# Step sizes and decays of a selective scan: their place in a two-layer diffusion block

## The chip, the core and the metric

The kernel runs on one core of a Trainium2 chip. The metric is the device time of one execution in microseconds (us), the median of several runs. Engines are named as in the profile: PE (TensorE's matmuls), PEld (its weight loads), DVE (VectorE), ACT (ScalarE), POOL (GpSimd), SP (the queue that issues most DMAs).

## What is computed

Two layers over 1024 latent tokens and 256 context tokens of width 1024. Each layer: modulated RMS norm, one input projection whose columns feed three head groups (latent attention, a bidirectional selective scan, windowed attention), one output projection, and a gated convolutional MLP. The part that matters here is the scan's:

```python
    xbc = jax.nn.silu(dwconv(xbc, conv_w, conv_b))
    xs, bm, cm = split_cols(xbc, (SSM_D_INNER, SSM_GROUPS * SSM_STATE, SSM_GROUPS * SSM_STATE))
    dt = jax.nn.softplus(dt_raw.astype(jnp.float32).reshape(b, l, 2, SSM_HEADS)
                         + dt_bias.astype(jnp.float32))
...
    xdt = (x.astype(f32) * dt[..., None]).reshape(b, nc, q, g, r, p)
    acs = jnp.cumsum((dt * a).reshape(b, nc, q, g, r), axis=2)
...
    a_last = acs[:, :, -1]
    states = jnp.einsum('bcqgn,bcqgr,bcqgrp->bcgrpn', bc, jnp.exp(a_last[:, :, None] - acs), xdt)

    def carry(hs, inp):
        st, al = inp
        return hs * jnp.exp(al)[..., None, None] + st, hs
...
    y_off = jnp.einsum('bcqgn,bcgrpn,bcqgr->bcqgrp', cc, h_start, jnp.exp(acs))
...
    y_diag = jnp.einsum('bcgqk,bcgrqk,bckgrp->bcqgrp', cb, decay, xdt)
```

Here `dt` are the step sizes, `acs` the decays summed within a chunk. There are 10 chunks of 128 tokens (2 of the context, 8 of the latent tokens), two directions and 6 heads: 12 step sizes per token. Everything runs in float32; matmuls of the projections are split into high and low halves, three products each.

## The kernel before

PE's instructions stand in the order in which the program text issues them. DVE, ACT, POOL and SP are ordered by the tile scheduler, which goes by a model of times. The text interleaves two streams: a *foreground* of projection products, and *background* generators. `bg(gen, delay)` queues a generator; each foreground product calls `tick()`, which resumes a generator when the modelled PE time has passed its due time; a `yield x` asks for x us of modelled PE time until the next resumption, with the numbers of the table `PACE` (one value for each layer). `drain()` runs what is left.

One layer's first half runs so in `body`:

- `w_in_ssd` (a generator) first makes the tile `krdt` (32 rows of a shared rotary key and 12 rows of raw step sizes, 1280 tokens wide) and the scan's gate `z`. Then it applies the rotary step in place to `krdt`: a shuffle L790 and a product L791 on DVE, a product L792 on POOL, the add L793 on DVE. It yields `krdt`.
- `next(w_in)` then makes the `xbc` columns: 7 groups of 128 channels, each a product over token chunks of 512, 512 and 256 (24 matmuls for each chunk, `p`), a convolution (DVE L508, ACT L512), transposes `ptr` and `px` and a spill to DRAM. In layer 0 the generator `early()` runs beside it: modulation vectors, long chains on DVE over tiles `wm` (L352, L354), transposes `pt` on PE, reductions L361. `drain()` ends this part, and the pool TD closes, whose place the scan's pool M takes.
- Then `side()` is queued as background: `ssd` (the scan), `scan_norm`, and `swa` (the windowed attention). The foreground goes on with `last_z` (the last columns of the gate), `w_in_att` (columns of the attentions), `mla_proj` (latent queries, keys, values) and `mla_att` (the heads of the latent attention).
- `drain()`, then `w_out` and the MLP.

`ssd` begins with the step sizes of all chunks: ten transposes `pdt` of `krdt`, the bias (L822), a softplus by a series on DVE (L828 to L839, with ACT's L825 and L826), a yield of 22, `dta` (L842), three matmuls `pacs` (the sums of the decays in both directions), copies L848 to L850, a yield, the transpose `pacT` and the DMA to `acsd` (L855), a few operations up to `wst` (L863), a yield, and then the scan: first the backward states (`xw` on POOL, L874, and the products `pst`), then for each chunk forward `pcb` and `py`. The results `dt`, `bias_`, `etot`, `wst` lie in a tile of pool M (tag "small"), the temporaries in a tile `sml2` of the pool U, which has 23 slots of 5 KB per partition.

Of the kernel before, what the change touches and what calls it, by code (L numbers as in the profile page):

```python
# [9 lines left out]
F32 = mybir.dt.float32  # L10
# [49 lines left out]
def _rope_tables():  # L60
# [21 lines left out]


PACE = {
    'dt': (22.0, 22.0),
    'back0': (4.0, 4.0),
    'back': (3.0, 3.0),
    'cb': (0.5, 0.5),
# [26 lines left out]
class Emit:  # L115
# [359 lines left out]

    def wk(self, w, M=128):
        return tuple([t[:, k, 0:M] for k in range(t.shape[1])] for t in w)

    def proj(self, w, x, chunks, M, put):

        ws = self.wk(w, M)
        for (s, e) in chunks:
            p = self.f("p")
            self.prod(ws, x, p[:M, 0:e - s], (s, e))
            put(p, s, e)

    def proj2(self, wps, x, chunks, need=None):

        for (s, e) in chunks:
            for ch in (CHUNKS[:1] if s == 0 else CHUNKS[1:]) if need else ():  # L490
                need(ch)
            ps = [self.f("p") for _ in wps]
            self.prods([self.wk(w, M) for w, M, _ in wps], x, [p[:M, 0:e - s] for p, (_, M, _) in zip(ps, wps)], (s, e))
            for p, (_, _, put) in zip(ps, wps):
# [65 lines left out]
    def up_names(self, l, u):  # L560
        return ("11", "12", "21", "22") if u < 2 else ("11", "12", "22", *(("21",) if l == 0 else ()), "S1", "S2", "S4", "S3")

    def up_weights(self, l):
# [10 lines left out]
        def make(u, name):  # L574
            def get():
# [8 lines left out]
                if name == "S1":  # L584
                    nc.vector.tensor_sub(a11, a11, a21)
                    nc.vector.tensor_add(a21, a21, a22)
                    raw = a21
                elif name == "S2":
                    nc.vector.tensor_sub(a22, a22, a11)
# [210 lines left out]
        return h, lo  # L800


    def ssd(self, l, krdt, out):
        nc, c = self.nc, l == 0
        sm = self.small[l]
        es = ExitStack()
        M = PoolTags(es.enter_context(self.tc.tile_pool(name=f"M{l}", bufs=1, reuse_waits="tile")),
                     {"small": 1, "fm": 2, "tm": 3, "ab": 4, "L": 3, "xw": 2, "cb": 2, "hf": 2, "hb": 2, "z": 2, "t": 1})
        S_ = M.tile([128, 4, 120], F32, tag="small", name=self.nm("sml"))
        dt, bias_, etot, wst = [S_[:, i, :] for i in range(4)]  # L810
        S2 = self.u(shape=[128, 10, 128], name="sml2")
        dta, tot, de, t1, av, t2 = [S2[:, i, 0:120] for i in range(6)]
        acs = de
        aexp, aT = S2[:, 6, 0:12], S2[0:120, 7, :]
        triF, triB = S2[:, 8, :], S2[:, 9, :]
        self.tri(triF, 0)
        self.tri(triB, 1)
        c3 = lambda ap: ap.rearrange("p (c j) -> p c j", j=12)
# [29 lines left out]
        nc.vector.tensor_copy(c3(acs)[:, :, 0:6], c3(p1[:, 0:120])[:, :, 0:6])  # L848
        nc.vector.tensor_copy(c3(acs)[:, :, 6:12], c3(p1[:, 120:240])[:, :, 6:12])
        nc.vector.tensor_copy(tot, p1[:, 240:360])  # L850
        yield 2.0
        p2 = self.b("pacT")
        self.tr(p2[:120, 0:128], acs)
        nc.vector.tensor_copy(aT, p2[:120, 0:128])
# [7 lines left out]
        nc.scalar.activation(etot, tot, AF.Exp)  # L862
        nc.vector.tensor_mul(wst, de, dt)  # L863

        yield 2.0

        def load_tm(k):
            t = M.tile([128, 5, 128], F32, tag="tm", name=self.nm("tm"))
# [3 lines left out]
        def weigh(tm, k, d):  # L872
            xw = M.tile([128, SH, SP], F32, tag="xw", name=self.nm("xw"))
            nc.gpsimd.tensor_tensor(out=xw, in0=tm[:, 0:3, :].rearrange("p i (h d) -> p (i h) d", d=SP),  # L874
                                    in1=c3(wst)[:, k, d * 6:d * 6 + 6].unsqueeze(2).to_broadcast([128, SH, SP]), op=ALU.mult)
            return xw
# [18 lines left out]
        xw = weigh(tms[0], order[0], 1)  # L895
        yield PACE['back0'][l]
        for i, k in enumerate(order):
            hn = M.tile([128, 384], F32, tag="hf", name=self.nm("hb"))
            tm, xk = tms.pop(0), xw
            if tms:  # L900
                xw = weigh(tms[0], order[i + 1], 1)
# [110 lines left out]
        hf = None  # L1012
# [5 lines left out]
        for i, k in enumerate(order):  # L1018
            hf = main(k, hf)
# [551 lines left out]
    def ffn(self, l, x, norm, feed, start=lambda: None, before_last=lambda: None):  # L1571
# [17 lines left out]
        def weight(u, name):  # L1589
            U_ = unit(u)  # L1590
            while name not in U_.w:
                U_.w[U_.names.pop(0)] = self.wnext(ahead=6)
            return U_.w[name]
# [24 lines left out]
        def step(u, s):  # L1618
# [22 lines left out]
            elif s == "6":  # L1641
                product(weight(u, "S2"), B["T2"], U_.X, False)
                put(U_, 0, 1, U_.X)
# [308 lines left out]
    def body(self):  # L1952
        tc, nc = self.tc, self.nc
        self.setup()
        self.C2 = PoolTags(self.ctx.enter_context(tc.tile_pool(name="c2", bufs=2)), {"r": 3, "vst": 1, "rr": 2, "edge": 2, "mx": 2, "mr": 2,
                             "sink": 1, "smx": 1, "smr": 1})
        self.W = PoolTags(self.ctx.enter_context(tc.tile_pool(name="W", bufs=2)), {"wst": 2, "whi": 3, "wlo": 3})
        self.U = PoolTags(self.ctx.enter_context(tc.tile_pool(name="U", bufs=2)), {"u": 23})
        self.PS = PoolTags(self.ctx.enter_context(tc.tile_pool(name="ps", bufs=2, space=PSUM)), {"f": 5, "b": 3})

        def xpool(l):
            es = ExitStack()
            p = es.enter_context(tc.tile_pool(name=f"X{l}", bufs=1, reuse_waits="tile"))
            self.X = PoolTags(p, {"x": 8, "ft": 1, "wm": 2, "pn": 1} if l == 0 else {"x": 9, "wm": 2})
            return es

        xs = xpool(0)
        self.wspec = self.layer_weights(0)
        x, h, need = self.start()
        for l in range(DEPTH):  # L1970
            c = l == 0
            chunks = CHUNKS if c else CHUNKS[:2]
            Y, hl, out = {}, {}, {}
            out["vst"] = self.C2.tile([128, NCH], F32, tag="vst", name=self.nm("vst"))
            self.zdone = False
            w_in = self.w_in_ssd(l, h, need)
            krdt = next(w_in)
            for f in range(KT):
                nc.sync.dma_start(out=self.spill[f], in_=x[f])
            xs.close()  # L1980
            with ExitStack() as es:
                self.TD = PoolTags(es.enter_context(tc.tile_pool(name=f"TD{l}", bufs=1, reuse_waits="tile")), {"t": 2, "tt": 2, "wm": 6})
                if c:
                    def early():
                        wt = lambda shape, name="wm": self.TD.tile(shape, F32, tag="wm", name=self.nm(name))
                        yield from self.mods_v(0, range(4, 12), wt, 3.0)
                        yield from self.load_params(1, wt)
                    self.bg(early())
                next(w_in)
                self.drain()  # L1990

            def side():
                self.scan = True
                yield from self.ssd(l, krdt, out)
                self.scan = False
                self.bg(self.scan_norm(l, Y, out["vst"]), PACE['sn0'][l])
                yield from self.swa(l, Y)
                while not self.ready:
                    yield 2.0
                for i in (6, 7):  # L2000
                    self.mix(l, Y, i, hl, i in (4, 1))

            self.ready, self.paced = False, True
            self.bg(side())
            next(w_in)()
            kva, qn = self.w_in_att(l, h)
            kbuf, qh, load, maxes = self.mla_loads(l)
            vt = self.mla_proj(l, kva, qn, kbuf, qh, load, maxes)

            def last():  # L2010
                self.ready = True
                for i in (3, 4, 5, 0, 1):
                    self.mix(l, Y, i, hl, i in (4, 1))

            finish = self.mla_att(l, vt, kbuf, qh, load, maxes, Y, last)
            self.drain()
            self.paced = False
            xs = xpool(l + 1)
            self.wspec = self.ffn_weights(l) + (self.layer_weights(l + 1) if l + 1 < DEPTH else [])
            x = []  # L2020
            norm = UpNorm(self, x, l, 1, chunks)
            self.w_out(l, Y, hl, finish, x, norm)
            x = []
            if l + 1 < DEPTH:
                tags = ["wm", "x"]

                def xw(shape):
                    tags.reverse()
                    return self.X.tile([128, NT] if tags[0] == "x" else [128, SEQ], F32, tag=tags[0], name=self.nm("wm"))[:, 0:SEQ].rearrange("p (k n) -> p k n", k=2)

                def xa(shape):
                    return self.X.tile(shape, F32, tag="wm", name=self.nm("wm"))

                def mods():
                    yield from self.mods_v(l + 1, range(12), xw, 4.6, xa, lambda n: 2 if n < 4 else 1)
                    self.gated = True

                self.gated = False
                nxt = Norm(self, x, l + 1, 0, CHUNKS, CHUNKS[:2])
                self.ffn(l, x, norm, nxt.feed, lambda: self.bg(mods(), 4.0), lambda: self.until(lambda: self.gated))  # L2040
                h, need = (nxt.hi, nxt.lo), nxt.need
            else:
                feed = self.final(x)
                self.ffn(l, x, norm, feed)
                self.drain()
        xs.close()
# [179 lines left out]
```

## Time and profile before

| | us |
|---|---|
| median of 3 runs | 3265.73 (3264.34 to 3267.45) |
| the profiled execution | 3266.09, of which the span is 3264.4 |
| PE busy | 3050.7 (93%) |
| DVE busy | 2132.6 (65%) |
| ACT busy | 1272.8 (39%) |
| POOL busy | 613.3 (19%) |

The profile is one execution. The span runs from the first to the last instruction; what is left of the execution's time, 1.7 us, lies around it. A share of the span is a mean over stages with different limits, so the rows below are read by stage. In rows of single instructions the bracket holds the idle time of that engine just ahead of the instruction, and what ended it. PEclk is the clock granted to TensorE, as a share of its full 2.4 GHz.

### The profile page before, as it was taken

What the parts mean: (1) busy time and instruction counts of PE and PEld (TensorE: products, weight loads), DVE (VectorE), ACT (ScalarE), POOL (GpSimd) and SP (SyncE); (2) the same over time, 40 slices, a digit from 0 to 9 for tenths busy, and PEclk for the clock granted to TensorE, in tenths of its full rate; (3) what the DMA queues carried; (4) which work ended last, traced back from release to release, by engine and by line L of the source; (5) the groups of instructions that cost most, each with busy time, mean ns of one, the idle gap of its engine ahead of it and who ended that gap; (6) DMA issues with size and microseconds to landing.
All of it is one profiled execution on the core that took longest, in us unless ns stands there. A gap on an engine that the chain in (4) does not pass through costs nothing.

```text
span 3264.4 us, 40114 instructions
## 1 busy us (share of the span) xinstructions
PE 3050.7 (93%) x15345; PEld 2402.0 (74%) x15345; DVE 2132.6 (65%) x3159; ACT 1272.8 (39%) x2204; POOL 613.3 (19%) x382
## 2 busy tenths in 40 slices
PE   6989978997999999997999999888999999999998
PEld 4878754554878888886888788655556778888887
DVE  4984887775285566668875734878653677677644
ACT  5433543443263343343111533553342444444212
POOL 2104633544100000000001303544453000000001
PEclk9989988998999999998999999988999999999999
DMA  8765666102202212227552445655113122225321
GB/s 269 221 188 156 211 216 173 39 15 95 96 30 73 79 58 71 78 67 285 176 166 78 130 115 164 215 173 149 42 42 97 62 78 78 90 84 180 130 74 62
DMA packets 349249, 392.42 MB, mean 120 GB/s; under 512 B 37203, under 2 KB 276452, under 8 KB 349057
## 3 DMA queue, kind: packets, MB, share of 16 engines
q1 hardware_dynamic: 348092, 389.62, 37.6%
q8 instruction: 121, 1.98, 0.3%
q0 software_dynamic: 704, 0.14, 0.1%
q14 instruction: 72, 0.58, 0.1%
q10 hardware_dynamic: 260, 0.10, 0.0%
HBM read 284.48 MB, written 104.01 MB: 119 GB/s over the span
## 4 chain that ended last, share of the span: by engine, by line
PE 77%; DVE 15%; DMA 3%; issue 2%; ACT 2%; POOL 1%; SPq 0%; DVEq 0%; ACTq 0%; POOLq 0%
PE p L143 34%; PE X L143 10%; PE Z L143 7%; PE s L143 6%; PE py L143 5%; PE pc L143 4%; PE V L143 3%; PE Y L143 3%; DVE wm L354 2%; DVE mx L1357 1%; PE pm L143 1%; PE pn L143 1%; PE pst L143 1%; DVE xbc L508 1%; DMA wm<-in_w_mod_dram 1%
## 5 line engine op out<-in xcount | busy, mean ns | idle before, releaser
L143 PE MATMUL p<-gh,wb 128*128 128x512 f32 (+1 forms) x1760 | 505.4, 371 | 0.0
L436 ACT CAST wb<-w 128x512 fp32r<-128x512 f32 (+1 forms) x412 | 251.5, 613 | 590.9 <-PE p L143 311.1
L437 DVE TENSOR_TENSOR wb<-w,wb 128x512 fp32r<-128x512 f32 (+1 forms) x412 | 279.4, 680 | 238.0 <-ACT wb L436 237.1
L143 PEld LDWEIGHTS p<-gh,wb 128*128 128x128 f32 x1760 | 321.1, 190 | 56.0 <-issue 0.2
L1567 DVE SCALAR_TENSOR_TENSOR x<-p,modT,x 128x512 f32<-128x512 f32 (+1 forms) x280 | 193.2, 695 | 243.8 <-PE p L143 243.5
L143 PE MATMUL X<-hb,wb 128*128 128x512 f32 x1440 | 340.4, 390 | 1.6 <-DVE cm L1605 1.6
L143 PE MATMUL p<-gl,wb 128*128 128x512 f32 (+1 forms) x880 | 325.7, 370 | 0.3 <-DVE gl L1746 0.3
L143 PEld LDWEIGHTS X<-hb,wb 128*128 128x128 f32 x1440 | 270.2, 188 | 58.3 <-DVE cm L1605 2.5
L143 PE MATMUL p<-hhi,wh 128*128 128x512 f32 (+1 forms) x792 | 290.9, 375 | 5.5 <-ACT z L643 3.3
L143 PE MATMUL p<-hlo,wh 128*128 128x512 f32 (+3 forms) x792 | 288.9, 366 | 2.6 <-POOL hlo L2128 1.8
L143 PE MATMUL p<-hhi,wl 128*128 128x512 f32 (+1 forms) x744 | 272.2, 366 | 2.5 <-DVE wl L424 2.3
L143 PE MATMUL Z<-hb,wb 128*128 128x512 f32 x960 | 233.0, 392 | 3.8 <-ACT cm L1607 3.8
L1441 ACT ACTIVATE P<-s 128x512 f32<-128x512 f32 x240 | 142.4, 597 | 239.5 <-PE s L143 236.1
L2074 POOL TENSOR_TENSOR acc<-acc,sq 128x512 f32<-128x512 f32 x24 | 32.8, 1371 | 1031.9 <-ACT sq L2073 1031.9
L143 PEld LDWEIGHTS Z<-hb,wb 128*128 128x128 f32 x960 | 180.1, 189 | 41.2 <-ACT cm L1607 4.7
L1448 POOL TENSOR_TENSOR acc<-acc,P 128x1024 f32<-128x1024 f32 x69 | 168.6, 2444 | 186.0 <-ACT P L1441 162.0
L143 PEld LDWEIGHTS p<-gl,wb 128*128 128x128 f32 x880 | 167.0, 190 | 28.1 <-DVE gl L1746 0.8
L354 DVE SCALAR_TENSOR_TENSOR wm<-wm,mstat,wm 128x512 f32<-128x512 f32 x224 | 161.6, 753 | 28.0 <-DMA wm<-in_w_mod_dram 27.5
L143 PEld LDWEIGHTS p<-hhi,wh 128*128 128x128 f32 x792 | 150.9, 191 | 31.2 <-ACT z L643 4.1
L143 PE MATMUL py<-P,vt 128*64 128x512 f32 (+3 forms) x744 | 173.4, 582 | 0.0
L143 PEld LDWEIGHTS p<-hlo,wh 128*128 128x128 f32 (+1 forms) x792 | 149.3, 188 | 26.0 <-POOL hlo L2128 2.7
L143 PEld LDWEIGHTS p<-hhi,wl 128*128 128x128 f32 x744 | 142.2, 191 | 26.5 <-DVE wl L424 3.2
(397 smaller groups left out, 5984.4 us busy)
## 6 DMA issues: line engine op xcount, KB each, us to landing
wm<-in_w_mod_dram SPq DMA_DIRECT2D x96, 512.0 KB
w<-in_ffn_w_up_dram SPq DMA_DIRECT2D x88, 512.0 KB
w<-in_ffn_w_down_dram SPq DMA_DIRECT2D x32, 512.0 KB
w<-in_w_in_dram SPq DMA_DIRECT2D x30, 512.0 KB
gd<-ft SPq DMA_DIRECT2D x22, 640.0 KB
gr<-gd SPq DMA_DIRECT2D x22, 640.0 KB
ab<-acsd SPq DMA_DIRECT2D x36, 384.0 KB
tm<-tmd SPq DMA_DIRECT2D x38, 320.0 KB
```

Of the source, the lines that this page charges most:

```text
L143: self.nc.tensor.matmul(out=out, lhsT=lhsT, rhs=rhs, start=start, stop=stop, **kw)
L354: nc.vector.scalar_tensor_tensor(out=acc[:, v, :], in0=w[:, i, :], scalar=c, in1=acc[:, v, :], op0=ALU.mult, op1=ALU.add)
L436: self.nc.scalar.copy(t[:, 0], raw)
L437: self.nc.vector.tensor_sub(t[:, 1], raw, t[:, 0])
L508: nc.vector.scalar_tensor_tensor(out=dst[:, d0:d1], in0=src, scalar=w, in1=dst[:, d0:d1], op0=ALU.mult, op1=ALU.add)
L1357: nc.vector.tensor_reduce(out=m[:, j, s:s + 1], in_=p, axis=AXX, op=ALU.max)
L1441: nc.scalar.activation(P[:, q * 512:(q + 1) * 512], s, AF.Exp, scale=sc)
L1448: (nc.vector if kt in ((2, 4, 6, 8) if self.scan else (4, 7)) else nc.gpsimd).tensor_add(acc, acc, P)
L1567: self.nc.vector.scalar_tensor_tensor(out=t[:, s:e], in0=p[:, 0:e - s], scalar=self.mcol(l, v, m)[:, o:o + 1], in1=t[:, s:e], op0=ALU.mult ...
L2074: (nc.gpsimd if self.n[ch] < 6 else nc.vector).tensor_add(acc, acc, sq[:, :n])
```

## The change

The part of `ssd` that makes step sizes and decays becomes a generator of its own, `ssd_dt`, and is queued as background ahead of the `xbc` columns of the same layer with a delay of 4. Its results go to a tile `sml` of pool U (instead of pool M), together with six of the former temporaries; two triangular masks and two small tiles stay in `sml2`, which is smaller. Two yields have new values (30 and 16 us for layers 0 and 1 in place of 22; 6 and 5 in place of 2), and the last yield of 2 is gone. `ssd` takes the results from `out["dt"]`.

```diff
 PACE = {
-    'dt': (22.0, 22.0),
+    'dt': (30.0, 16.0),
+    'dt2': (6.0, 5.0),
...
-    def ssd(self, l, krdt, out):
+    def ssd_dt(self, l, krdt, out):
+
         nc, c = self.nc, l == 0
         sm = self.small[l]
-        es = ExitStack()
-        M = PoolTags(es.enter_context(self.tc.tile_pool(name=f"M{l}", bufs=1, reuse_waits="tile")),
-                     {"small": 1, "fm": 2, "tm": 3, "ab": 4, "L": 3, "xw": 2, "cb": 2, "hf": 2, "hb": 2, "z": 2, "t": 1})
-        S_ = M.tile([128, 4, 120], F32, tag="small", name=self.nm("sml"))
-        dt, bias_, etot, wst = [S_[:, i, :] for i in range(4)]
-        S2 = self.u(shape=[128, 10, 128], name="sml2")
-        dta, tot, de, t1, av, t2 = [S2[:, i, 0:120] for i in range(6)]
+        S_ = self.u(shape=[128, 10, 128], name="sml")
+        dt, bias_, etot, wst, dta, tot, de, t1, av, t2 = [S_[:, i, 0:120] for i in range(10)]
+        out["dt"] = dt, bias_, etot, wst
+        S2 = self.u(shape=[128, 4, 128], name="sml2")
...
-        yield 2.0
+        yield PACE['dt2'][l]
...
         nc.vector.tensor_mul(wst, de, dt)
 
-        yield 2.0
+    def ssd(self, l, out):
+        nc, c = self.nc, l == 0
+        sm = self.small[l]
+        es = ExitStack()
+        M = PoolTags(es.enter_context(self.tc.tile_pool(name=f"M{l}", bufs=1, reuse_waits="tile")),
+                     {"fm": 2, "tm": 3, "ab": 4, "L": 3, "xw": 2, "cb": 2, "hf": 2, "hb": 2, "z": 2, "t": 1})
+        dt, bias_, etot, wst = out["dt"]
...
                     self.bg(early())
+                self.bg(self.ssd_dt(l, krdt, out), 4.0)
                 next(w_in)
                 self.drain()
 
             def side():
                 self.scan = True
-                yield from self.ssd(l, krdt, out)
+                yield from self.ssd(l, out)
```

Where the instructions stand. First PE in layer 0, where the first chunk of the `xbc` columns (`p_885`, 24 matmuls) ends; `krdt_461` is the tile of raw step sizes. Before:

```order
320 L143 MATMUL p_885<-hhi_581,wh_625 128x512
321 L143 MATMUL p_885<-hlo_582,wh_625 128x512
322 L143 MATMUL p_885<-hhi_581,wl_626 128x512
323 L143 MATMUL p_927<-hhi_396,wh_625 128x512
324 L143 MATMUL p_927<-hlo_397,wh_625 128x512
```

And in the changed kernel:

```order
320 L144 MATMUL p_885<-hhi_581,wh_625 128x512
321 L144 MATMUL p_885<-hlo_582,wh_625 128x512
322 L144 MATMUL p_885<-hhi_581,wl_626 128x512
323 L149 MATMUL pdt_927<-ident,krdt_461 128x44 x10
324 L144 MATMUL p_972<-hhi_396,wh_625 128x512
325 L144 MATMUL p_972<-hlo_397,wh_625 128x512
```

The ten transposes stood at row 839, behind the first matmuls of last_z; now they stand between the first two chunks of the columns. The matmuls `pacs` moved from row 951 to row 484, and `pacT` from 962 to 525.

Second, DVE at the same place. The row of `krdt_461<-krdt_461,sh_854` is the add that ends the rotary step. Before:

```order
101 L508 SCALAR_TENSOR_TENSOR xbc_877<-p_927,prm_172,xbc_877 128x511
102 L354 SCALAR_TENSOR_TENSOR wm_1040<-wm_1088,mstat,wm_1040 128x512 x2
103 L352 TENSOR_SCALAR wm_1200<-wm_1201,mstat 128x512 x2
104 L508 SCALAR_TENSOR_TENSOR xbc_877<-p_964,prm_172,xbc_877 128x255
105 L793 TENSOR_TENSOR krdt_461<-krdt_461,sh_854 32x1024
106 L508 SCALAR_TENSOR_TENSOR xbc_877<-p_927,prm_172,xbc_877 128x511
```

In the changed kernel, from the same place to the first operation on `pdt`:

```order
101 L355 SCALAR_TENSOR_TENSOR wm_1076<-wm_1127,mstat,wm_1076 128x512 x2
102 L353 TENSOR_SCALAR wm_1230<-wm_1231,mstat 128x512 x2
103 L794 TENSOR_TENSOR krdt_461<-krdt_461,sh_854 32x1024
104 L355 SCALAR_TENSOR_TENSOR wm_1076<-wm_1127,mstat,wm_1076 128x512 x2
105 L355 SCALAR_TENSOR_TENSOR wm_1230<-wm_1231,mstat,wm_1230 128x512 x2
106 L355 SCALAR_TENSOR_TENSOR wm_1076<-wm_1164,mstat,wm_1076 128x512
107 L800 TENSOR_TENSOR kpl_860<-krdt_461,kph_859 32x1280
108 L821 TENSOR_TENSOR sml_923<-pdt_927,sm_185 128x120
```

The two convolution operations at 101 and 104 moved behind the add; the chain of the step sizes begins at row 108 and ends with `dta` at row 199, with operations on `wm` between all of its steps.

Third, PE in layer 0 at the last forward chunk of the scan (its `pcb` is the third row of either listing). Before:

```order
1702 L143 MATMUL py_4040<-ab_3818,hb_3820 64x128 x2
1703 L143 MATMUL py_4040<-L_3879,tm_3812 64x128 x2
1704 L143 MATMUL pcb_4066<-fm_4017 128x128 x2
1705 L143 MATMUL pr_4090<-identr,mr_4006 1x128 x2
1706 L143 MATMUL s_4098<-qh_3343,kh_3339 128x512
```

In the changed kernel:

```order
1577 L144 MATMUL py_3718<-ab_3473,hb_3477 64x128 x2
1578 L144 MATMUL py_3718<-L_3529,tm_3469 64x128 x2
1579 L144 MATMUL pcb_3744<-fm_3690 128x128 x2
1580 L144 MATMUL pv_3762<-wh_3133,kvh_2317 128x384
1581 L144 MATMUL pv_3762<-wl_3134,kvh_2317 128x384
```

The last chunk stood directly ahead of the first scores of the latent attention (`s`); now products of `mla_proj` (`pv`, and `p` behind them) follow it.

## Rows read from the trace of the kernel before

**Rows 1.** Page, part 1 (busy us, share, instructions) and the chain of waits by engine.

```profile
PE 3050.7 (93%) x15345; PEld 2402.0 (74%) x15345; DVE 2132.6 (65%) x3159; ACT 1272.8 (39%) x2204; POOL 613.3 (19%) x382
...
PE 77%; DVE 15%; DMA 3%; issue 2%; ACT 2%; POOL 1%; SPq 0%; DVEq 0%; ACTq 0%; POOLq 0%
```

**Rows 2.** Busy time by stretch, layer 0's columns; the first line names the columns.

```profile
core 0: us, PE busy (x) PEld busy (x) DVE busy (x) ACT busy (x) POOL busy (x), PEclk, DMA share, GB/s
100.00:150.00 50.00, 49.15 (x268) 41.98 (x266) 50.00 (x81) 16.53 (x26) 6.41 (x3) 1.00 0.78 235
150.00:200.00 50.00, 49.58 (x279) 42.04 (x279) 50.00 (x91) 17.41 (x28) 0.00 (x0) 1.00 0.80 240
```

**Rows 3.** Tile `krdt` in layer 1: ns min/median/max, first and last start us.

```profile
L793 DVE TENSOR_TENSOR krdt<-krdt,sh x1: 1208/1208/1208, 1861.6 to 1861.6; 32x1024 f32<-32x1024 f32 x1
```

**Rows 4.** Single instructions, PE and DVE, layer 0: start, us, [idle before <-releaser].

```profile
103.01 0.39 PE L143 MATMUL p<-hhi,wl 128*128 128x512 f32 x1
103.24 0.39 PE L143 MATMUL p<-hhi,wh 128*128 128x512 f32 x1
...
118.36 1.20 DVE L793 TENSOR_TENSOR krdt<-krdt,sh 32x1024 f32<-32x1024 f32 x1
...
215.18 1.09 PE L148 MATMUL pt<-ident,wm 128*128 128x128 f32 x4 [6.64 <-DVE wm L354]
...
223.60 1.94 PE L148 MATMUL pt<-ident,wm 128*128 128x128 f32 x8 [6.48 <-DVE wm L354]
...
225.57 0.78 PE L143 MATMUL p<-hhi,wh 128*128 128x512 f32 x1
```

**Rows 5.** DVE groups by shape, 100 to 226 us: count, busy us, mean ns.

```profile
L354 DVE SCALAR_TENSOR_TENSOR wm<-wm,mstat,wm 128x512 f32<-128x512 f32 x101 | 71.6, 753 | 0.0
L508 DVE SCALAR_TENSOR_TENSOR xbc<-p,prm,xbc 128x511 f32<-128x511 f32 x28 | 20.4, 730 | 0.0
...
L361 DVE TENSOR_REDUCE modT<-pt 128x4 f32<-128x512 f32 x16 | 10.5, 672 | 0.8 <-PE pt L148 0.8
L508 DVE SCALAR_TENSOR_TENSOR xbc<-p,prm,xbc 128x255 f32<-128x255 f32 x14 | 6.5, 465 | 0.0
L352 DVE TENSOR_SCALAR wm<-wm,mstat 128x512 f32<-128x512 f32 x12 | 5.2, 467 | 0.0
```

**Rows 6.** Tile `sml`, 226 to 260 us; last, the POOL operation behind it.

```profile
L835 DVE TENSOR_TENSOR sml<-sml x9: 282/284/286, 232.6 to 237.2; 128x120 f32<-128x120 f32 x9
L836 DVE TENSOR_SCALAR sml<-sml x9: 222/223/224, 232.9 to 237.5; 128x120 f32<-128x120 f32 x9
...
L829 DVE RECIPROCAL sml<-sml x1: 890/890/890, 231.1 to 231.1; 128x120 f32<-128x120 f32 x1
...
258.54 2.60 POOL L874 TENSOR_TENSOR xw<-tm,sml 128x384 f32<-128x384 f32 x2 [37.36 <-DVE sml L863]
```

**Rows 7.** Busy time by stretch at the start of last_z.

```profile
225.00:231.00 6.00, 6.00 (x24) 4.67 (x23) 2.26 (x8) 2.12 (x4) 0.00 (x0) 0.50 0.91 311
231.00:240.00 9.00, 9.00 (x39) 7.39 (x38) 6.63 (x25) 1.65 (x2) 0.00 (x0) 0.96 0.02 6
```

**Rows 8.** Busy time by stretch: w_in_att, mla_proj, first heads, tail of layer 0.

```profile
261.00:350.00 89.00, 89.00 (x524) 76.40 (x523) 49.87 (x69) 35.83 (x79) 45.44 (x38) 0.96 0.58 165
370.00:450.00 80.00, 60.68 (x406) 50.36 (x404) 77.24 (x123) 43.55 (x115) 36.25 (x26) 0.91 0.79 249
450.00:490.00 40.00, 30.87 (x179) 21.41 (x179) 30.57 (x45) 16.73 (x32) 15.78 (x8) 0.83 0.55 169
490.00:510.00 20.00, 10.88 (x32) 5.61 (x33) 19.88 (x21) 6.13 (x9) 8.32 (x3) 0.57 0.75 256
740.00:765.00 25.00, 14.87 (x72) 8.33 (x70) 15.34 (x8) 11.49 (x17) 17.79 (x7) 0.80 0.00 1
```

**Rows 9.** Single PE instructions, tail of layer 0 and start of w_out.

```profile
760.90 1.12 PE L143 MATMUL pd<-acc,ones 128*64 128x512 f32 x2 [10.13 <-POOL acc L1178]
...
796.58 0.80 PE L143 MATMUL p<-mixh,wh 128*128 128x512 f32 x1 [6.42 <-ACT wh L423]
```

**Rows 10.** Layer 1: one PE instruction, then busy time by stretch (columns, scan).

```profile
1862.08 0.39 PE L143 MATMUL p<-hhi,wh 128*128 128x512 f32 x1
...
1900.00:1955.00 55.00, 55.00 (x289) 46.89 (x288) 20.13 (x35) 22.10 (x35) 0.00 (x0) 1.00 0.44 125
...
2050.00:2120.00 70.00, 57.81 (x363) 46.88 (x362) 57.23 (x85) 35.73 (x90) 38.59 (x26) 0.95 0.77 238
2120.00:2180.00 60.00, 51.38 (x304) 39.09 (x304) 48.30 (x87) 33.22 (x85) 24.75 (x16) 0.89 0.68 222
2180.00:2260.00 80.00, 67.92 (x286) 38.30 (x284) 62.40 (x76) 27.67 (x44) 35.87 (x15) 0.83 0.59 169
```

More of the change, by code (lines that the diff above doesn't have):

```diff
@@ L800, in split @@
         return h, lo
-    def ssd(self, l, krdt, out):
+    def ssd_dt(self, l, krdt, out):
         nc, c = self.nc, l == 0
         sm = self.small[l]
-        es = ExitStack()
-        M = PoolTags(es.enter_context(self.tc.tile_pool(name=f"M{l}", bufs=1, reuse_waits="tile")),
-                     {"small": 1, "fm": 2, "tm": 3, "ab": 4, "L": 3, "xw": 2, "cb": 2, "hf": 2, "hb": 2, "z": 2, "t": 1})
-        S_ = M.tile([128, 4, 120], F32, tag="small", name=self.nm("sml"))
-        dt, bias_, etot, wst = [S_[:, i, :] for i in range(4)]
-        S2 = self.u(shape=[128, 10, 128], name="sml2")
-        dta, tot, de, t1, av, t2 = [S2[:, i, 0:120] for i in range(6)]
+        S_ = self.u(shape=[128, 10, 128], name="sml")
+        dt, bias_, etot, wst, dta, tot, de, t1, av, t2 = [S_[:, i, 0:120] for i in range(10)]
+        out["dt"] = dt, bias_, etot, wst
+        S2 = self.u(shape=[128, 4, 128], name="sml2")
         acs = de
-        aexp, aT = S2[:, 6, 0:12], S2[0:120, 7, :]
-        triF, triB = S2[:, 8, :], S2[:, 9, :]
+        aexp, aT = S2[:, 0, 0:12], S2[0:120, 1, :]
+        triF, triB = S2[:, 2, :], S2[:, 3, :]
         self.tri(triF, 0)
@@ L863, in ssd @@
         nc.vector.tensor_mul(wst, de, dt)
-        yield 2.0
+    def ssd(self, l, out):
[5 more added lines that the diff above has]
+        dt, bias_, etot, wst = out["dt"]
+        c3 = lambda ap: ap.rearrange("p (c j) -> p c j", j=12)
         def load_tm(k):
```

## Prediction

> **What bounds the kernel now.** I read the engine shares first. TensorE (PE) is busy 93% of the span and the chain of waits is 77% PE [rows 1]: the kernel is one hand-written PE order, and a change is worth the PE idle time (and low granted clock) that it removes or makes. So I read PE's idle stretches and asked in each which engine ends the wait. Four places matter.
>
> First, the columns of layer 0's input projection. VectorE (DVE) is busy 50.00 us of every 50 there, with the modulation vectors of `early()`, while PE is dense at clock 1.00 [rows 2]. PE pays only at the end: two waits of 6.64 and 6.48 us, both ended by the last `wm` operations, and then a start of last_z at half clock [rows 4, 7]. Second, layer 0's scan beside mla_proj: 370 to 510 us, where DVE is nearly full and PE is idle for 37.6 of 140 us [rows 8]. Third, layer 0's tail, where PE waits 10.13 us for GpSimd's (POOL) accumulation and the clock is 0.80 [rows 8, 9]. Fourth, the same scan in layer 1: 2050 to 2260 us, with PE idle for 33 us at clocks of 0.95 to 0.83 [rows 10].
>
> **Where the step sizes go in layer 0: two new waits of PE.** PE runs its order strictly. In the trace four transposes wait 6.64 us with ready matmuls behind them, and nothing passes [rows 4]. The Trainium skill, page TensorE: Matmul & The Clock Gate, section The mechanism, says the same: matmuls start and end in program order. Were it otherwise the next two terms would be nearly nothing; the trace decides for the order.
>
> The ten transposes `pdt` stand right behind the first chunk of 24 matmuls. They read all 44 rows of `krdt`, and so they need the rotary step in place, whose last operation is the add L793 on DVE. PE begins the second chunk at 103.24 [rows 4]; the add starts at 118.36 and takes 1.20 [rows 4]. In the new DVE order two convolution operations ahead of it go behind it (0.73 + 0.47 us [rows 5]), because their matmuls now come later. So it ends at about 118.4, and PE waits 118.4 − 103.4 = 15 us. It could be 12 if the scheduler's order is kept more loosely, and no more than 16.
>
> Then DVE must run the chain of the step sizes among the modulation work. Between the add and `dta` the new order has 55 `wm` operations of 753 ns, 8 of 467, 8 + 4 convolution operations of 730 and 465, four reductions of 672 [rows 5], nine pairs of 284 + 222 and a reciprocal of 890 [rows 6], and some 6 us of others: 41.4 + 3.7 + 5.8 + 1.9 + 2.7 + 4.6 + 0.9 + 6 = 67 us. The durations of [rows 5] overlap by some 8% (they add up to about 136 us in a stretch of 126), so I take 62: `dta` ends at 118.4 + 62 = 180. PE gets to `pacs` after 153 matmuls, which last some 33 us at full clock, plus the transposes and a slow start: 118.6 + 1.3 + 33 + 3 = 156. It waits 24 us (15 if the durations are the short ones, 30 if they don't overlap).
>
> After a long wait the granted clock is 0.50 for about 6 us [rows 7], about 3 us of work each time, so 6 for two waits. On the other side the modulation work is done while PE waits: the last `wm` operation now stands ahead of the last two column groups, so the waits of 13.1 us at the end and the slow start there (3 us) go. Sum up to last_z: 15 + 24 + 6 − 13 − 3 = **+29 us** (+17 to +36). The ten transposes, three matmuls and one transpose only move.
>
> **What is queued behind.** Every column group waits with PE, and ScalarE's and DVE's convolutions after it. The scan's first state product needs `xw` from POOL, which needs the `tm` loads; these wait for the TD pool, which closes at the end of the columns. In the new order that product stands only some 5 us of matmuls behind last_z's start. I allow **+1.5 us** (0 to 3). POOL, which idled 37.36 us for the chain before [rows 6], is ready. The one DMA that moves, `acsd`, has no reader before the forward scan. The tile `sml` now holds one of 23 slots of the U pool through the scan; the rotation of w_in_att's tiles gets shorter by one. Nothing in the trace prices that; PE is dense there (89.00 of 89 us [rows 8]), so I take nothing, up to 5.
>
> **What is given back.** The scan no longer waits for its step sizes, so its chunks stand earlier against the foreground. Counting only projection matmuls from last_z on, at 0.227 us per 512 columns [rows 4], the first forward chunk stood at 58 us and now at 33, the last at 131 and now at 117. Each chunk now stands where the chunk three before it stood, and the last no longer sits at the very end of mla_proj with its partners bunched 6 and 4 us apart. In absolute time the scan starts as before (about 258); what is different is that some 28 us of w_in_att is still to be done then, which leaves DVE half free (49.87 of 89 us [rows 8]).
>
> *Layer 0, 370 to 510.* Idle 37.6 us; lost clock 0.09 × 60.7 + 0.17 × 30.9 + 0.43 × 10.9 = 15 us [rows 8]; together 53. Three chunks of ten leave it, at no gain for the rotations of the windowed attention at 490 to 510, which stay where they are. Somewhat under a third: **−16 us** (−4 to −26).
>
> *Layer 0's tail.* The windowed attention ends one head earlier, so that POOL's long sums stand further from the end. The wait of 10.13 and a little clock go: **−11 us** (0 to −14). What is late next is the 6.42 us wait for the weights of w_out [rows 9], which stays.
>
> *Layer 1.* No modulation work stands beside the columns: DVE is busy 20.13 of 55 us [rows 10]. The add of the rotary step starts at 1861.6 [rows 3], just as PE leaves its first chunk at about 1862 [rows 10]: a wait of 0.7 us, and up to 1 at `pacs`. There the shift is nearly free. 2050 to 2260 holds 33 us of idle and about 0.05 × 57.8 + 0.11 × 51.4 + 0.17 × 67.9 = 20 us of lost clock. A quarter of 53, less 1.5: **−12 us** (+2 to −22).
>
> **Sum:** +29 + 1.5 − 16 − 11 − 12 = −8.5 us against the profiled run's own 3266.09 (span 3264.4 and 1.7 around it; 0.4 above the median of 3265.73). That is 3257.
>
> **The rivals.** *Slower: the stalls of layer 0 are not won back.* Its place is PE's two waits behind DVE's modulation queue, its price the +29. It decides when the three later places together give back less than 30: if the chunks only trade with other DVE work, the mixer gives 5, the tail 8 and layer 1 5. That is 29 + 1.5 − 18 = +12.5, so 3279; with the longer second wait and w_in_att's tiles late, 3286. For it speaks that both waits are read from full DVE windows, while each gain is a share of a stretch with many waiters. *Faster by more:* the second wait is 15, the scan's stretches lose half of their loss in both layers: 20 + 1.5 − 26 − 12 − 22 = −38, so 3228. For it speaks that three of ten chunks go where DVE is half free. *No change:* the terms cancel to within 6.5 us, which is also about what a measurement tells from no change (0.2%); 3266. *It does not do what it says:* PE need not wait, because the new steps slip behind the modulation work; against it stands the written PE order, and it falls into the case before.
>
> **How the numbers follow.** Forecast 3257, with its neighbourhood from 3240 to 3259: 0.35. Slower: 0.28. Faster by more: 0.15. No change: 0.22. Faster 0.35 + 0.15 = 0.50, same 0.22, slower 0.28. The range holds the bounds with a tenth cut on either side: 3228 to 3286.
>
> **What would show it.** Right: in layer 0 PE waits about 15 us for `pdt`, ended by the add of `krdt`, and some 24 for `pacs`, ended by DVE; last_z starts near 254; no wait for `wm` at the end; less than 30 us of PE idle where the scan meets mla_proj; no 10 us wait for POOL in the tail; in layer 1 the two new waits are under 2 us. Wrong: the wait for `pacs` is under 10 or over 35 us, or the stretch beside mla_proj keeps its 38 us of idle, or the tail's wait comes back with another releaser.

## The result and the profile after

The changed kernel took 3311.34 us (median of 4 runs, 3310.12 to 3316.79) against 3265.52 for the kernel before: a ratio of 1.0138, 95% interval 1.012 to 1.0155. It is slower by 46 us, outside the range.

In the table, `last_z` and `w_out` stand for the first matmul of each, and the rotary step is the shuffle on `krdt`. All are start times in us of the two profiled executions.

| | before | after | later by |
|---|---|---|---|
| layer 0: last_z | 225.57 | 251.90 | 26.3 |
| layer 0: w_out | 796.6 | 839.1 | 42.5 |
| layer 1: rotary step of `krdt` | 1854.4 | 1895.6 | 41.2 |
| layer 1: w_out | 2470.6 | 2514.6 | 44.0 |
| end of the span | 3264.4 | 3308.9 | 44.5 |

So the loss is layer 0's, in two parts: 26.3 us up to last_z, where +29 was predicted, and 16 us from there to w_out, where −25.5 was predicted. Layer 1 loses 3 us in place of gaining 12.

The first part is as predicted, and answers [rows 4]. The page's engine line, PE's waits from 90 to 340 us (us in total, times, longest), and three stretches: one with the first wait in it, one with the second, and the 6.5 us behind the second:

```profile
PE 3054.6 (92%) x15345; PEld 2404.3 (73%) x15345; DVE 2126.1 (64%) x3156; ACT 1273.3 (38%) x2204; POOL 606.5 (18%) x385
```

```profile
PE pacs L144 <- DVE sml L856: 23.3, 1, 23.3
PE pdt L149 <- DVE krdt L794: 15.2, 1, 15.2
PE pst L144 <- POOL xw L880: 5.8, 1, 5.8
PE p L144 <- ACT z L644: 3.1, 1, 3.1
```

```profile
103.00:118.90 15.90, 0.69 (x4) 0.23 (x3) 15.90 (x21) 1.82 (x2) 5.34 (x3) 0.59 0.77 227
160.00:177.50 17.50, 0.03 (x1) 0.06 (x1) 16.12 (x36) 0.01 (x1) 0.00 (x0) 0.50 0.45 135
177.50:184.00 6.50, 6.50 (x27) 5.59 (x28) 6.17 (x14) 2.36 (x4) 0.00 (x0) 0.73 0.54 164
```

PE waits 15.2 us for the rotary add and 23.3 us for `dta` (L841, which ends at 177.3; the profile puts the wait down to L856, the next row of DVE), while DVE (the third busy column) is full or nearly so. Behind the second wait the granted clock is 0.73 for 6.5 us. The two waits for `wm` at the end are gone, and the first state product waits 5.8 us for its loads.

The second part is new. Whole stretch from last_z to w_out, before and then after (us, busy PE, PEld, DVE, ACT, POOL, PEclk, DMA share, GB/s):

```profile
225.50:796.60 571.10, 503.07 (x2744) 348.26 (x2742) 396.71 (x559) 247.89 (x486) 261.07 (x144) 0.93 0.43 130
```

```profile
251.90:839.10 587.20, 510.79 (x2726) 351.95 (x2725) 375.41 (x525) 240.33 (x478) 250.06 (x145) 0.92 0.42 128
```

The stretch is 16.1 us longer: 8.4 us more PE idle (76.4 in place of 68.0) and 7.7 more busy, for a little less work at a lower clock. DVE has 21 us less to do and still the gain didn't come. PE's waits from 456 to 516 us, where the scan ends beside mla_proj, say which one is new. Before:

```profile
PE pr L143 <- DVE sink L1059: 6.5, 1, 6.5
PE py L143 <- ACT z L998: 4.3, 1, 4.3
PE pm L143 <- DVE mx L1357: 1.7, 1, 1.7
```

After:

```profile
PE pm L144 <- DVE ql L1217: 11.3, 1, 11.3
PE pr L144 <- DVE mr L1369: 5.9, 1, 5.9
PE py L144 <- ACT z L1004: 4.0, 1, 4.0
PE pm L144 <- DVE vt L1295: 2.4, 1, 2.4
```

`ql` is the low half of a latent query, an operation of mla_proj. DVE's instructions ahead of it (start, us, [idle before <-releaser]), then PE's and ACT's at the same time:

```profile
491.03 0.69 DVE L1363 TENSOR_REDUCE mx<-pm 128x1 f32<-128x512 f32 x1 [0.51 <-PE pm L144]
494.72 0.01 DVE L791 LOAD_MASK_SELECT sh<-swr  x1 [3.00 <-DMA swr<-swd]
494.74 1.29 DVE L791 STREAM_SHUFFLE sh<-swr 128x1024 f32<-128x1024 f32 x1
496.06 1.23 DVE L792 TENSOR_TENSOR sh<-sh,sin 128x1024 f32<-128x1024 f32 x1
499.52 1.23 DVE L794 TENSOR_TENSOR swr<-swr,sh 128x1024 f32<-128x1024 f32 x1 [2.23 <-POOL swr L793]
502.07 1.49 DVE L1056 TENSOR_TENSOR swl<-swr,swh 128x1280 fp32r<-128x1280 f32 x1 [1.32 <-ACT swh L1055]
503.49 0.02 DVE L791 LOAD_MASK_SELECT sh<-swr  x1
503.49 1.28 DVE L791 STREAM_SHUFFLE sh<-swr 128x1024 f32<-128x1024 f32 x1
504.66 0.67 DVE L1217 TENSOR_TENSOR ql<-p,qh 64x512 fp32r<-64x512 f32 x1
```

```profile
493.82 0.28 PE L144 MATMUL p<-qn,wl 128*64 128x256 f32 x1
505.39 0.80 PE L144 MATMUL pm<-kh,qh 96*128 96x512 f32 x1 [11.29 <-DVE ql L1217]
```

```profile
500.78 1.26 ACT L1055 CAST swh<-swr 128x1280 fp32r<-128x1280 f32 x1 [8.75 <-DVE swr L794]
501.94 1.32 ACT L1216 CAST qh<-p 64x512 fp32r<-64x512 f32 x3
```

PE made the products for `ql` at about 493. DVE is idle for 6.5 us between 491 and 505, some 4 of them while PE waits, but `ql` stands in its queue behind a rotation of the windowed attention (the rotary step of a tile `swr` of its queries or keys), which waits in turn for a load, for POOL and for ACT. The same rotation holds ACT up: `qh`, the high half that `ql` reads, is cast only at 501.94, behind the cast of the rotated tile (`swh`), for which ACT was idle for 8.75 us. So `ql` stood behind the rotation in two queues, and PE waits for all of it. The loads (DMA share 0.84 from 483 to 506) come late too. Before the change the rotations began behind the last `ql`.

### The profile page after: what moved, and what is told of

Same layout as the page of the kernel before. It is cut to its first block, busy times and chain, and to the rows that moved or that the text cites. A ratio compares the mean times of both kernels' runs of the same rounds, so it can differ in the third digit from the quotient of the medians.

```text
span 3308.9 us, 40119 instructions
## 1 busy us (share of the span) xinstructions
PE 3054.6 (92%) x15345; PEld 2404.3 (73%) x15345; DVE 2126.1 (64%) x3156; ACT 1273.3 (38%) x2204; POOL 606.5 (18%) x385
## 4 chain that ended last, share of the span: by engine, by line
PE 77%; DVE 13%; DMA 4%; issue 3%; ACT 2%; POOL 1%; SPq 0%; DVEq 0%; POOLq 0%; ACTq 0%
PE p L144 34%; PE X L144 10%; PE Z L144 7%; PE s L144 5%; PE py L144 5%; PE pc L144 4%; PE V L144 3%; PE Y L144 3%; DVE wm L355 1%; DVE mx L1363 1%; PE pm L144 1%; PE pn L144 1%; DVE acc L1398 1%; DMA xr<-in_x_dram 1%; PE pst L144 1%
```

## The experiments

The theories were these. **A**: the loss is PE's two waits in layer 0's columns; the earlier scan costs (A1) or is neutral (A2). **B**: the slot of pool U that `sml` holds has a price. **C**, formed after the first eight runs (the expectation of `hold` had named the rotations under A1): the earlier scan pulls the rotations ahead of mla_proj's last operations on DVE. Times are medians; a ratio is to the kernel before on the same chip, with its 95% interval.

### Which layer

`l1only`: layer 0 makes the chain at the start of the scan again, with the old yields; `l0only`: layer 1 does.

```diff
...
-                self.bg(self.ssd_dt(l, krdt, out), 4.0)
+                if l == 1:
+                    self.bg(self.ssd_dt(l, krdt, out), (4.0, 4.0)[l])
...
+                if l == 0:
+                    yield from self.ssd_dt(l, krdt, out)
+                    yield 2.0
                 yield from self.ssd(l, out)
```

> Layer 0 makes its step sizes at the start of the scan again, with the old yields; layer 1 keeps them early; the tile sml is in pool U in both layers. Theory A (the loss is PE's two waits in layer 0's columns, and the earlier scan gives nothing back): layer 1's part alone is worth about +3 us, so 3265 to 3272. Theory B (the slot of pool U that sml holds slows the scan and the rotations of both layers): layer 0 keeps some 10 to 15 us of its loss too, so 3275 to 3285. My prediction's layer 1 term (-12) would give 3254.

> Layer 0 early as in the change, layer 1 at the start of the scan with the old yields; sml in pool U in both. Theory A: all but about 3 us of the loss stays, 3305 to 3310. Theory B: 3308 to 3315, since the slot is held in layer 1 as well. If layer 1's early chain itself loses, 3300.

`l1only`: 3277.37 us, 1.0034 (1.0023 to 1.0045). `l0only`: 3310.80, 1.0134 (1.0118 to 1.0149). Layer 0 holds nearly the whole loss. But 11 us stay without it, 8 of them in layer 0 up to w_out (804.7 against 796.6), where only the place of `sml` differs: more than A allows, and a first sign for B.

### The two waits

`late0`: layer 0's chain stands later within the columns.

```diff
-    'dt': (30.0, 16.0),
+    'dt': (70.0, 16.0),
...
-                self.bg(self.ssd_dt(l, krdt, out), 4.0)
+                self.bg(self.ssd_dt(l, krdt, out), (24.0, 4.0)[l])
```

> The change with layer 0's chain later within the columns: delay 24 in place of 4, first yield 70 in place of 30, so that PE meets pdt 20 us and pacs 54 us of projection matmuls later; layer 1 and the early scan as in the change. Theory A: both waits (15.2 and 23.3 us) go; VectorE's total work then ends the columns, about 10 us later than before the change; last_z starts near 236 in place of 251.9, and the time is 3292 to 3298. If the two waits were only a symptom, 3308 to 3313.

3291.23 us, 1.0080 (1.0057 to 1.0104). PE's waits from 90 to 250 us:

```profile
PE pacs L144 <- DVE sml L856: 11.8, 1, 11.8
PE pst L144 <- POOL xw L880: 5.9, 1, 5.9
PE pt L149 <- DVE wm L355: 4.5, 2, 3.1
```

The wait for `pdt` is gone; that for `pacs`, expected to go too, is halved. last_z starts at 232.5, 19.4 us earlier than in the change, and the time falls by 20.1 (19 by the ratios, whose interval here is 8 us to either side): what the columns lose arrives at the end about one for one. Of the 7 us that stay against 225.57, 3 are waits (11.8 for `pacs` and 4.5 for `wm`, where 13.1 stood before). 25 us of the loss stay, 18 of them behind last_z.

### The slot of pool U

`uslot`: the kernel before, with the tile in U instead of M. `copym`: the change, with a copy into M at the start of the scan. `late0copym`: `late0` with the same copy.

```diff
...
+        S_ = M.tile([128, 4, 120], F32, tag="small", name=self.nm("sml"))
+        nc.vector.tensor_copy(S_, out["sml"][:, 0:4, 0:120])
+        dt, bias_, etot, wst = [S_[:, i, :] for i in range(4)]
```

> The kernel before with one change: the tile of step sizes and decays lies in pool U (as in the change) and not in pool M; both layers make it at the start of the scan, with the old yields. PE's order is that of before, row for row. Theory B (the slot of U has a price of its own): by layer 0 of the run with only layer 1 early (8.1 us longer up to w_out than before) and layer 1 of the run with only layer 0 early (2.3 longer), 3274 to 3278. If the slot is free and those differences came from elsewhere: 3264 to 3268.

> The change, but at the start of the scan the four results are copied (one VectorE operation of 128 x 480) into a tile of pool M, and the slot of U is free from then on. Theory B: the slot's 8 + 2 us come back, 3299 to 3304. Theory A alone (waits and shift): 3309 to 3313, the copy's half microsecond at worst.

> As the run with layer 0's chain later in the columns (no waits of PE for pdt and pacs), with the copy into pool M as well. Theories A and B together: 3291 less the slot's 10, 3279 to 3284; what is then left over before (13 to 18 us) is 7 us of VectorE's longer queue in layer 0's columns and the price of the earlier scan. Theory A alone: 3289 to 3293. If the earlier scan were the gain that I predicted, the three together would come to 3250.

`uslot`: 3271.99 us, 1.0017 (1.0008 to 1.0026). `copym`: 3305.08, 1.0128 (1.0112 to 1.0143). `late0copym`: 3286.43, 1.0062 (1.0048 to 1.0076). By the ratios the slot costs 6, 3 and 6 us, less than the 10 that B expected. Only `uslot` against before is clear of its interval. In its profiled execution the loss lies in layer 0 (581.1 us from last_z to w_out against 571.0 before), while layer 1 is 4 us shorter. PE's order is that of before, but not all else is: the first cast of `qn` on ACT starts at 372.2 us in place of 365.7. What comes late for want of the slot was not followed further.

### The place of the scan

`hold`: the change with a yield of 26 ahead of the scan. `late0h13` and `late0h22`: `late0copym` with yields of 13 and 22 there. `l1m`: layer 0 as before, layer 1 early with the copy; `l1mhold`: the same with the scan of layer 1 held by 26.

```diff
+                yield (26.0, 26.0)[l]
                 yield from self.ssd(l, out)
```

> The change with a yield of 26 us of modelled PE time ahead of the scan in both layers, so that the scan's chunks stand against the foreground about where they stood before the change (first forward chunk 69 us of projection matmuls ahead of the first scores in layer 0, 72 before); the step sizes stay early. Theory A1 (the earlier scan pushes the rotations of the windowed attention into mla_proj and loses there): the two waits' +26 us stay and the rest goes, 3288 to 3296. Theory A2 (the earlier scan is neutral): 3305 to 3315. Theory B (slot of pool U): 3305 to 3312, since the slot is held even longer.

> The same base, with the scan held by 13 us of modelled PE time in both layers: half of the shift is undone, the last forward chunk stands 4 us of projection matmuls ahead of the first scores in layer 0 (14 in the change, 0 before). Theory A1 (the price grows with the shift, about 8 us in layer 0 and 3 to 5 in layer 1 for the half): 3277 to 3282. If the place of the scan is not what costs: 3284 to 3289.

> The same base with the scan held by 22 us: its forward chunks stand in layer 0 exactly where they stood before the change (72.4 us of projection matmuls ahead of the first scores down to 0). Theory A1: what is left is the 8 us by which last_z starts later, 3270 to 3277. If the place of the scan is not what costs: 3284 to 3289. The run that held the scan by 26 us, 3 us later than before, lost more in layer 0 than the shift did, which speaks for the second.

> Layer 0 exactly as before, layer 1 as in the change (early chain, early scan) but with the copy into pool M. Against the run that also held layer 1's scan (3265.8) it prices the earlier scan in layer 1 alone. My prediction: -12, 3254. Theory C: +3 to +6, 3268 to 3272. Neutral: 3264 to 3267.

> Layer 0 exactly as before; layer 1 with the early chain, the copy into pool M, and the scan held back by 26 us of modelled PE time, so that its chunks stand against the foreground where they stood before. What is left of the change is that ten microseconds of VectorE's chain and its two waits move from w_in_att into the columns of layer 1. Layer 1 was 6.4 us shorter than before in the run that held the scan. If that is the worth of the move, 3257 to 3261, faster than before; if it was chance of alignment, 3264 to 3268.

| | us | ratio (95%) |
|---|---|---|
| `hold` | 3301.85 | 1.0105 (1.0088 to 1.0122) |
| `late0copym`, no hold | 3286.43 | 1.0062 (1.0048 to 1.0076) |
| `late0h13` | 3271.01 | 1.0012 (1.0003 to 1.0022) |
| `late0h22` | 3282.94 | 1.0043 (1.0029 to 1.0057) |
| `l1m` | 3268.69 | 1.0006 (0.9996 to 1.0015) |
| `l1mhold` | 3265.80 | 1.0002 (0.9993 to 1.0011) |

In layer 1 the early chain is worth nothing, with its scan early or held. In layer 0 the place of the scan matters, by 15 us for a hold of 13, but not in one direction: A1's price growing with the shift falls, and A2 with it. `late0h22` is not settled: two of its ten executions, the profiled one among them, took 3268 to 3269 us, the others 3280 to 3286. I have no trace of the longer kind. `hold` fell into none of its three ranges and is no clean return either: its scan stood 3 us of matmuls later than before, its last `pcb` waited 9.8 us for a load, and it lost more behind last_z than the change (593.1 us to w_out against 587.2). In it the rotations begin at 518 us, well behind the last `ql` at 467, and PE waits 15.6 us in total for a result of the windowed attention (`smr`): a windowed attention that comes too late has a price too.

### The rotations

`late0sw`: `late0copym` with one line ahead of the windowed attention, which leaves the scan early. `aftsw`: the change itself with that line. `befsw`: the kernel before with it.

```diff
+                yield 26.0
                 yield from self.swa(l, Y)
```

> The run with the later chain and the copy, with a yield of 26 us of modelled PE time ahead of the windowed attention in both layers: the scan keeps its early place, the three rotations of the windowed attention go back behind mla_proj. Theory C (the early scan costs because the rotations' VectorE operations, waiting for swr loads and POOL, stand ahead of mla_proj's ql in VectorE's queue: 16.5 us of PE's waits for ql in that run): the waits for ql fall under 4 us, and the time to 3272 to 3281. If the rotations only pass the wait on to the heads (sink and mr, 13 us before the change), 3282 to 3290.

> The change itself with one line more: a yield of 26 us of modelled PE time ahead of the windowed attention in both layers. Chain, scan and the tile in pool U stay as in the change, and so do the waits of PE for pdt and pacs. Theory C (what was lost behind last_z is the rotations ahead of mla_proj's ql in VectorE's queue): about the 24.5 us that the same line gave on the base without the waits, 3285 to 3292; the waits for ql (11.3 + 3.1 us in layer 0) fall under 7. If the line only worked together with the later chain or the copy: 3300 to 3312.

> The kernel before with the same line ahead of the windowed attention, and nothing else. If the line were a gain of its own, whatever the step sizes do: 3240 to 3260. Theory C says that before the change the rotations stand behind mla_proj anyway, so that the line only delays the windowed attention into the end of the layer: 3266 to 3290.

`late0sw`: 3261.86 us, 0.9986 (0.9975 to 0.9996), 24.6 less than its base (25 by the ratios); C expected less of a gain, and a wait for `ql` under 4 us, where 6.5 stay. `aftsw`: 3286.81, 1.0073 (1.0058 to 1.0088), 24.5 less than the change (21 by the ratios). `befsw`: 3276.05, 1.0035 (1.0022 to 1.0047), 12.5 more than before. The line gains on two bases and loses where the rotations already stood behind mla_proj, so it is no gain of its own. It moves the whole windowed attention, not the rotations alone, and it does so in both layers. PE's waits in `aftsw` from 251 to 830 us:

```profile
PE pr L144 <- DVE mr L1369: 11.6, 5, 6.2
PE pd L144 <- POOL acc L1184: 10.4, 2, 10.1
PE p L144 <- ACT wh L424: 6.7, 1, 6.7
PE pst L144 <- POOL xw L880: 5.7, 1, 5.7
PE p L144 <- DVE ql L1217: 4.3, 1, 4.3
```

The change has a second, shorter wait for `ql` beside the one of 11.3 us:

```profile
PE p L144 <- DVE ql L1217: 3.1, 1, 3.1
```

So the waits for `ql` fall from 14.4 to 4.3 us. The wait of 10.1 us in the tail of [rows 9] is back. That the two gains are so near to each other is in part chance: in the profiled executions layer 0's stretch from last_z to w_out gets 13.3 us shorter in `aftsw` (587.2 to 573.9) and 22.5 in `late0sw` (587.1 to 564.6); the rest of `aftsw`'s gain lies in layer 1 (6.4 us) and ahead of last_z (3.0).

### Sizing, and a version that is not slower

`late0sw14`: a yield of 14 in place of 26. `late0sw20h6`: the scan held by 6, the windowed attention by 20. `late0swb`: `late0sw` again. `late0mix`: in layer 1 the scan held by 13 and the windowed attention not held.

> The run with the later chain, the copy and the held windowed attention, with a yield of 14 in place of 26: the rotations begin about when mla_proj ends. Theory C: the waits for ql grow again with the overlap, while the tail of layer 0 (a wait of 10 us for POOL's sums at a hold of 26, 3.4 at none) improves; 3258 to 3275, nearer to the 26 if the rotations' place matters more than the tail.

> The same base, with the scan held by 6 us and the windowed attention by 20, so that it stands where it stood with 26, and PE no longer meets the first state product before its loads (a wait of 5.9 us for xw in layer 0). If that wait is worth its length: 3254 to 3260; if it is given back behind it: 3260 to 3266.

> The run with the later chain, the copy and the held windowed attention once more, unchanged, for a closer interval against the kernel before: 3259 to 3264 against 3264 to 3266, a ratio of 0.997 to 1.000. If its first measurement was a lucky chip, 3265 or more.

> The same in layer 0; in layer 1 the windowed attention is not held, but the scan by 13 us (the place in which layer 1 was shortest, 609 us from the rotary step to w_out against 615 to 616). If those 5 us were the place: 3253 to 3258. If they were scatter between executions: 3260 to 3266.

`late0sw14`: 3271.46 us, 1.0026 (1.0014 to 1.0037). `late0sw20h6`: 3265.00, 1.0003 (0.9994 to 1.0013). `late0swb`: 3261.48, 0.9990 (0.9981 to 0.9999). `late0mix`: 3262.83, 0.9991 (0.9982 to 1.0). Half the hold gives 15 of the 24.6 us (12 of 25 by the ratios). This parts C in two. With a hold of 14 the rotations already begin behind the last `ql` (478.8 against 464.8 us), and the waits for `ql` fall from 16.5 to 4.6 us, much as with 26 (6.5). Whole stretch from last_z to w_out in `late0copym` (no hold), `late0sw14` and `late0sw`, one execution each:

```profile
233.60:820.70 587.10, 513.77 (x2725) 355.10 (x2724) 378.76 (x527) 242.10 (x479) 251.25 (x145) 0.91 0.42 128
234.10:808.60 574.50, 511.41 (x2726) 350.58 (x2725) 391.45 (x528) 242.69 (x479) 257.12 (x145) 0.92 0.43 131
231.80:796.40 564.60, 497.53 (x2725) 343.28 (x2724) 383.76 (x529) 242.44 (x479) 259.93 (x145) 0.94 0.45 134
```

The first half of the hold takes 10 us of PE's idle time away, about what the waits for `ql` lost: that is the rotations ahead of `ql`. The second half takes none away; PE is busy for 14 us less with the same matmuls, at a clock of 0.94 in place of 0.92. (The profiled execution of `late0sw14` is its longest, 4.5 us above the median; the medians of the two lie 9.6 us apart.) That part lies among the heads, behind the rotations: from 600 to 700 us `late0sw14` runs 443 matmuls at a clock of 0.93, and `late0sw` 493 at 1.00.

```profile
600.00:700.00 100.00, 90.35 (x443) 52.53 (x442) 74.26 (x99) 36.91 (x67) 46.96 (x22) 0.93 0.16 40
600.00:700.00 100.00, 94.82 (x493) 56.69 (x492) 69.84 (x99) 44.10 (x78) 49.52 (x23) 1.00 0.14 35
```

Which of the windowed attention's later operations does this was not isolated.

In `late0sw20h6` the wait at the first state product falls from 5.9 to 2.8 us and others grow: it is not worth its length. `late0sw`, twice measured, beats the change by 1.5% and the kernel before by 0.10 to 0.14%, at the edge of what can be told. Its stretch of 564.6 us stands against 571.1 before and 587.2 in the change: the early scan's gain is there, and it is some 6 us. Three executions with this layer 0 took 564 to 565 us (`late0sw`, `late0swb`, `late0mix`), and three with layer 0 as before 571 to 573 (before, `l1m`, `l1mhold`).

## Why the prediction was wrong

**PE's two waits: right.** 15.2 and 23.3 us against 15 and 24, last_z 26.3 us later against 29, and the waits for `wm` gone. Counting DVE's queue from the order, with durations from the trace, held to a microsecond for both waits, the second with some luck: `dta` ended at 177.3 against 180, and PE came to `pacs` at 154 against 156, two errors of the same sign. The slow starts, +6 − 3 in the sum, were over-sized: 15.2 + 23.3 − 13.1 leave 0.9 us of the 26.3 for them.

**The first state product: under-sized.** 5.8 us against 1.5, with bounds 0 to 3. As `late0sw20h6` shows, a shorter wait there gives nothing at the end.

**The slot of U: under-sized.** I took 0, up to 5; three pairs of runs say 3 to 6. I argued from a dense PE in w_in_att, but the slot is held through the whole scan.

**Layer 0, 370 to 510: the step that failed.** The prediction said that the rotations of the windowed attention "stay where they are". They did not. I had read their place from PE's order, in which the windowed attention's first matmuls still stood behind mla_proj. A rotation has no PE instruction: it is DVE, POOL, ACT and SP work, and the generator reaches it as soon as the scan ends. DVE's order, which was at hand, shows it: before, the last `ql` stands 32 rows ahead of the first rotation,

```
456 L1211 TENSOR_TENSOR ql_3918<-p_3967,qh_3917 64x256
488 L790 STREAM_SHUFFLE sh_4247<-swr_4246 128x1024
```

and after the change, three rotations have begun ahead of the last three `ql`:

```
459 L791 STREAM_SHUFFLE sh_3960<-swr_3959 128x1024
474 L791 STREAM_SHUFFLE sh_4037<-swr_4036 128x1024
478 L791 STREAM_SHUFFLE sh_4092<-swr_4091 128x1024
479 L1217 TENSOR_TENSOR ql_4080<-p_4081,qh_4079 64x512
```

The stretch of [rows 8] from 370 to 510 us, moved on by last_z's 26.3 us, shows that nothing was given back in it:

```profile
396.30:536.30 140.00, 102.05 (x556) 81.29 (x556) 103.53 (x169) 55.97 (x129) 43.62 (x27) 0.82 0.76 243
```

PE is idle for 38.0 us, as against 37.6 before, which the prediction had named as a sign of being wrong. So the term of −16 was a loss. Holding the windowed attention back takes 21 to 25 us off (`aftsw`, `late0sw`). About half of that is the rotations ahead of `ql` (`late0sw14`); the other half hangs on where the rest of the windowed attention stands among the heads, and its cause stays open. What the earlier scan itself gave is some 6 us of the 27 forecast for layer 0.

**The tail: half right.** PE's waits after the change from 690 to 840 us, against [rows 9]:

```profile
PE s L144 <- DVE ya L1400: 5.6, 2, 5.3
PE pd L144 <- POOL acc L1182: 3.4, 1, 3.4
PE pr L144 <- DVE mr L1369: 3.3, 1, 3.3
...
PE p L144 <- ACT wh L424: 1.3, 1, 1.3
```

The wait for POOL fell from 10.1 to 3.4 us and that for w_out's weights, which was to stay, from 6.4 to 1.3, but DVE's `ya` and `mr` took 8.9 in their place.

**Layer 1: wrong.** The waits are small as predicted (0.7 us for `pdt`), but the shift gives nothing: `l1m` and `l1mhold` stand at 1.0006 and 1.0002. The 3 us that layer 1 loses in the table are within scatter: two executions of one kernel (`late0sw`, `late0swb`) differ by 5 us there.

**The sum.** From last_z to w_out layer 0 took 571.1 us before and 587.2 in the change. With the slot free it took 584.3 (`copym`), with the windowed attention held 573.9 (`aftsw`), with both 564.6 (`late0sw`, whose chain also stands later in the columns). So the early scan gave 6 us, and the slot and the place of the windowed attention took 23 together: 3 and 20, or 9 and 13, by which is put right first. With 26 up to last_z and 3 in layer 1, less 1 in the MLP between, that is the 44.5 of the span. These are single executions, so this is a check and no proof. My "slower" rival had the waits and "the chunks only trade with other DVE work", at a price of 12.5 to 20 us. It had the sign, not the mechanism. The shares that I gave (under a third in layer 0, a quarter in layer 1) rested on no row.

## What to carry to other kernels

When background work moves earlier, everything queued behind it moves too: look for the next stage's instructions on every engine, above all those with no instruction on the engine whose order you read. An operation that waits for a load can hold up what stands behind it in its queue, as the rotation did `ql` on DVE and `qh` on ACT, even on an engine that is half idle. An experiment that delays a whole stage prices the whole stage: it took a second, smaller delay to part the rotations from the rest. A wait of the bounding engine ahead of a stage can be counted from two orders and a table of durations; a gain taken as a share of a crowded stretch can't, and should carry both signs.

## What the runs showed that I had not expected

An engine need not be full to stop PE: in the change PE waited 11.3 us for DVE while DVE itself was idle for some 4 of them. One slot of 23 in pool U, held through the scan, costs 6 us with PE's order unchanged (`uslot`). In `late0sw` most of what the held windowed attention gave back was not idle time but clock: of layer 0's 22.5 us, 16 are PE's busy time for the same 2725 matmuls, at a granted clock of 0.94 in place of 0.91.
